# A pipelined scan in a decoder trunk: one pool of raw weights for the whole kernel, and another order of work at the scan's two ends

## The chip, the cores and the metric

The kernel runs on one core of one Trainium2 chip. The metric is device time in microseconds (us) for one execution, and the time given is the median of several executions. One execution is recorded by the hardware profiler; its rows give starts, durations and waits per engine: PE (TensorE), ACT (ScalarE), DVE (VectorE), POOL (GpSimd) and SP (SyncE, which here only issues DMAs).

## The reference

Two layers over 272 tokens (256 and 16 meta tokens) with a model width of 2048, all in float32. Layer 0 is RWKV-7 time mixing and SwiGLU, layer 1 stick-breaking attention and SwiGLU. The change lies in the time mixing:

```python
r = xr @ w_r
k = xk @ w_k
v = xv @ w_v
w = -jax.nn.softplus(-(dec_w0 + jnp.tanh(xw @ dec_w1) @ dec_w2)) - 0.5
decay = jnp.exp(-jnp.exp(w))
a = jax.nn.sigmoid(a_w0 + (xa @ a_w1) @ a_w2)
g = jax.nn.sigmoid(xg @ g_w1) @ g_w2
...
def step(state, inp):
    r_t, d_t, k_t, v_t, kk_t, a_t = inp
    sa = jnp.einsum('bhvk,bhk->bhv', state, -kk_t)
    state = (state * d_t[:, :, None, :]
             + sa[..., None] * (kk_t * a_t)[:, :, None, :]
             + v_t[..., None] * k_t[:, :, None, :])
    return state, jnp.einsum('bhvk,bhk->bhv', state, r_t)

_, y = lax.scan(step, s0, tuple(seq_first(t) for t in (rh, dh, kh, vh, kk, ah)))
...
out = ((y + bonus) * g) @ w_o
```

Behind it come `h = h + mix`, an RMS norm and `(silu(x @ w_gate) * (x @ w_up)) @ w_down`.

## The kernel before

**Weights.** Every weight matrix of 2048 x 2048 is read in 16 column blocks m of 16 row blocks k. A load brings eight blocks of 128 x 128 (512 KB) to a buffer of the pool `wraw`, called `raw`; half of it (four blocks, 128 x 512) is then split in two: ACT casts it to `whi` (fp32r), DVE subtracts to get `wlo`. The activations are split in the same way (`hl`, hi and lo). A block against the 272 tokens is then three matmuls in `mm3k` (lines 186 to 188): hi by hi, lo by hi, hi by lo. There are NWHL = 6 pairs of whi and wlo. The time mixing has NRAW = 3 raw buffers in a pool of its own, which is given back at its end; the rest of the kernel has a second pool of four.

**Stages, with their time in the profiled execution.** The norm, and then k = xk @ w_k (0 to 180 us): the first three column blocks in plain fp32 (line 472), the others split, with the small low-rank matrices (`dec_w1`, `a_w1`, `g_w1`) taken along by `rest()` between the blocks. The key of a block goes through ACT (`kt`, `xi`) to a small matmul `kq` (line 490), which prepares the keys' norm. The scan (180 to about 664 us). Then `wo_first`: the rest of `o @ w_o`, the residual `h` and its squares. From about 690 us FFN, attention and FFN.

**The scan** works on pairs of heads, 16 in all, in chunks of 64 tokens. In iteration n = -3 to 15, four pairs are in hand in different phases: C = pair n+3 (its low-rank terms, `lora`), B = pair n+2 (`chunk0`, `scores`, `solve`, `neg`, `bonus`, `tokens`, `values`), M = pair n+1 (`inverse`, `left`, `right`, `apply`, `trans`: the triangular inverse is done in two levels; its pieces go through DRAM, `s<-G`, `Tt<-s`), and A = pair n (`states`, four times `step`, then `norm` and `gate`, which gives the output o[n]). Between these small pieces `fill` takes steps from `stream`; a step is one weight block, three matmuls. The order of these calls in `scan` sets the order on every engine, and an engine serves its list in that order.

**The stream** delivers, pair by pair, 16 steps of w_v and 16 of w_r, and after the 512th the head of w_o: for m = 0 to 3 the k = 0 to KHEAD-1, as far as o[k] is done, into PSUM banks that stay open (`self.wo`). `chunks` loads its raws, NRAW ahead, and splits one half ahead of its use. The number of steps per iteration is 32; the last three iterations, with no C, call `fill(k / 2)`: 16 steps. 516 steps are taken before those, 48 in them, and 48 w_o steps (4 x 12) stand there.

**`wo_first`** loads k = 12 to 15 of m = 0 to 3 (four raws of 256 KB), does 16 blocks with them and goes on with m = 4 to 15, whose banks are taken in turn from the pool pmm.

SP issues the loads of raw weights, of the lora weights (`w<-lora`, `rn<-rkd`), the transfers through DRAM in the scan, and two stores that zero a DRAM scratch (`s<-zero`); `blk` is a small table of constants, of which ACT makes a scaled copy.

Of the kernel before, what the change touches and what calls it, by code (L numbers as in the profile page):

```python
# [26 lines left out]
C = 64  # L27
# [10 lines left out]
ALIAS = {"kk": "ld"}  # L38
NRAW = 3
NWHL = 6  # L40
NRAW2 = 4
G0 = 3
# [3 lines left out]
NXL = 7  # L46
LEAD = 4
PSTEP = 8
NHEAD = 4
KHEAD = 12  # L50
ASTRIDE = 2
# [67 lines left out]
class Builder:  # L119
# [89 lines left out]

    def proj(self, src, acts, nk=NK, m=128):  # L210
        w = self.weights(src, nk, m)
        out = self.mmbank()[:m, :acts[0][-1].shape[1]]
        for k in range(nk):
            self.mm3k(out, w[k], acts[k], k == 0, k == nk - 1)
        return out
# [45 lines left out]
    def build(self):  # L261
        tc, nc = self.tc, self.nc
        with ExitStack() as ctx:
# [13 lines left out]
            self.wx = None  # L277
            with ExitStack() as c2:
                self.wraw = c2.enter_context(tc.tile_pool(name="wraw", bufs=NRAW))
                self.time_mix()  # L280
            self.wide = True
            if self.stop == "tm":
                return
            with ExitStack() as c2:
                self.wraw = c2.enter_context(tc.tile_pool(name="wraw2", bufs=NRAW2))
                self.consts2 = c2.enter_context(tc.tile_pool(name="cp2", bufs=1)).tile(
# [64 lines left out]
    def time_mix(self):  # L351
# [13 lines left out]
        with ExitStack() as ctx:  # L365
# [8 lines left out]
            for i in range(2):  # L374
                st = {}
                for n, w in (("B0", 64), ("V0", 64), ("SC0", 128)):
                    st[n] = sp.tile([128, w], F32, name=f"{n}_{i}", tag=f"{n}_{i}")
                    nc.gpsimd.memset(st[n], 0.0)
                self.static.append(st)
                z = self.dram.tile([10, 65, 64], F32, name=f"s2_{i}", tag=f"s2_{i}", bufs=1)  # L380
                self.dq.dma_start(z.rearrange("s i t -> (s i t)").rearrange("(p x) -> p x", p=128),
                                  zero)
                self.s2.append(z)
            o, n = CONST["blk"]
            self.blk = [sp.tile([128, n], F32, name="blk", tag=f"blk{i}") for i in range(2)]
            self.dq.dma_start(self.blk[0], a["consts"][:, o:o + n])
            nc.scalar.activation(self.blk[1], self.blk[0], AF.Copy, scale=1.0 / HD)
# [218 lines left out]
    def scan(self, sp):  # L606
# [9 lines left out]
        stream = self.stream(pairs)  # L616
        left = [0]

        def fill(k):
# [7 lines left out]
        for n in range(-3, NK):  # L627
            get = lambda i: pairs.get(n + i)
            A, M, B, C = get(0), get(1), get(2), get(3)
            f = fill if C else lambda k: fill(k / 2)  # L630
            if M:
# [3 lines left out]
            if A:  # L635
                A.states()
                A.step(1)
            if B:
                B.chunk0()
# [15 lines left out]
            if B:  # L655
                B.bonus()
            f(2)
            if B:
                B.tokens()
            f(6 + (LEAD if n == -3 else 0))  # L660
            if B and n + 2 == NK - 1:
# [60 lines left out]
    def chunks(self, jobs):  # L722
# [6 lines left out]
        def load():  # L729
            if len(raws) < len(todo):  # L730
                src, j0, j1 = todo[len(raws)]
                raw = self.wraw.tile([128, (j1 - j0) * 128], F32, name="raw", tag="raw")
                nc.sync.dma_start(raw, src[:, j0 * 128:j1 * 128])
                raws.append(raw)

        def split(raw, k0, k1):
            n = (k1 - k0) * 128
            hi = self.whl.tile([128, n], F32R, name="whi", tag="whi")
            lo = self.whl.tile([128, n], F32R, name="wlo", tag="wlo")
            part = raw[:, k0 * 128:k1 * 128]  # L740
            nc.scalar.copy(hi, part)  # L741
            nc.vector.tensor_tensor(lo, part, hi.bitcast(F32), ALU.subtract)  # L742
            return [(hi[:, k * 128:(k + 1) * 128], lo[:, k * 128:(k + 1) * 128])
                    for k in range(k1 - k0)]

        for _ in range(NRAW):
            load()
        ahead = None
        for i, (src, j0, j1) in enumerate(todo):
# [9 lines left out]
    def stream(self, pairs):  # L759

        a = self.a
        w = self.chunks([(a[n][p], NK) for p in range(NK) for n in ("w_v", "w_r")]
                        + [(a["w_o"][m][:, :KHEAD * 128], KHEAD) for m in range(NHEAD)])
        for p in range(NK):
# [632 lines left out]
```

## Time and profile before

| | us |
|---|---|
| median of three runs | 2739.09 |
| the three runs | 2735.81, 2739.09, 2741.37 |
| the profiled execution | 2735.73 |
| its span, first to last instruction | 2733.9 |
| PE idle over the span | 67.5 |
| PE idle from 178 to 200 us | 10.4 |
| PE idle from 624 to 690 us | 12.6 |

Rows of the time line are: start, duration, engine, line, operation, output <- inputs, size, count, and in brackets the time that the engine stood idle before and what ended that. SPq and ACTq rows are DMAs being issued. A row that stands for several instructions has their number behind the x. A wait list has, for an engine and line, what it waited for: us in all, how often, the longest. A matmul's duration overlaps with its neighbours'; what counts is the time from one start to the next.

### The profile page before, as it was taken

What the parts mean: (1) busy time and instruction counts of PE and PEld (TensorE: products, weight loads), DVE (VectorE), ACT (ScalarE), POOL (GpSimd) and SP (SyncE); (2) the same over time, 40 slices, a digit from 0 to 9 for tenths busy, and PEclk for the clock granted to TensorE, in tenths of its full rate; (3) what the DMA queues carried; (4) which work ended last, traced back from release to release, by engine and by line L of the source; (5) the groups of instructions that cost most, each with busy time, mean ns of one, the idle gap of its engine ahead of it and who ended that gap; (6) DMA issues with size and microseconds to landing.
All of it is one profiled execution on the core that took longest, in us unless ns stands there. A gap on an engine that the chain in (4) does not pass through costs nothing.

```text
span 2733.9 us, 53852 instructions
## 1 busy us (share of the span) xinstructions
PE 2666.4 (98%) x20942; PEld 2464.4 (90%) x20942; DVE 1771.0 (65%) x3543; ACT 1470.0 (54%) x2943; POOL 167.0 (6%) x477
## 2 busy tenths in 40 slices
PE   6989999998999999999999999999999999999999
PEld 4878888887999999999999999988888888888888
DVE  6666666674655555555556775577766666666665
ACT  5665565654554444444445754477555455554553
POOL 0004333331000000000000000000000000000000
PEclk9999999998999999999999999999999999999999
DMA  5434343433655555555555545533555665665655
GB/s 176 137 108 123 92 119 98 119 86 109 197 176 165 185 177 163 186 177 164 185 176 167 181 162 170 170 116 108 186 185 181 197 188 178 198 190 179 199 178 179
DMA packets 185329, 439.50 MB, mean 161 GB/s; under 512 B 58448, under 2 KB 88688, under 8 KB 185072
## 3 DMA queue, kind: packets, MB, share of 16 engines
q1 hardware_dynamic: 183488, 433.63, 50.5%
q8 instruction: 164, 2.69, 0.4%
q10 hardware_dynamic: 1584, 2.42, 0.3%
q14 instruction: 93, 0.76, 0.1%
HBM read 430.24 MB, written 5.74 MB: 159 GB/s over the span
## 4 chain that ended last, share of the span: by engine, by line
PE 75%; DVE 0%; issue 0%
PE mm L192 22%; PE mm L186 13%; PE mm L188 13%; PE mm L187 13%; PE mm L191 11%; PE hms L869 1%; PE z L946 1%; PE lt L959 0%; PE op L970 0%; PE tbv L938 0%; PE op L971 0%; PE lt L960 0%; PE lt L962 0%; PE ms L801 0%; PE op L972 0%; DVE h L208 0%
## 5 line engine op out<-in xcount | busy, mean ns | idle before, releaser
L168 DVE TENSOR_TENSOR wlo<-raw,whi 128x512 fp32r<-128x512 f32 (+1 forms) x1448 | 978.9, 679 | 618.1 <-ACT whi L167 599.2
L167 ACT CAST whi<-raw 128x512 fp32r<-128x512 f32 (+1 forms) x1448 | 879.3, 610 | 870.8 <-PE mm L187 539.6
L186 PE MATMUL mm<-hl,whi 128*128 128x272 f32 x3344 | 982.5, 294 | 14.8 <-ACT whi L741 9.3
L188 PE MATMUL mm<-hl,wlo 128*128 128x272 f32 x3344 | 968.8, 290 | 4.6 <-DVE wlo L168 3.8
L187 PE MATMUL mm<-hl,whi 128*128 128x272 f32 x3344 | 965.8, 289 | 0.0
L192 PE MATMUL mm<-hl,whi 128*128 128x512 f32 x2624 | 919.9, 395 | 0.0
L191 PE MATMUL mm<-hl,wlo 128*128 128x256 f32 x2624 | 740.8, 282 | 0.0
L186 PEld LDWEIGHTS mm<-hl,whi 128*128 128x128 f32 x3344 | 632.0, 189 | 27.5 <-ACT whi L741 9.8
L187 PEld LDWEIGHTS mm<-hl,whi 128*128 128x128 f32 x3344 | 637.8, 191 | 1.9
L188 PEld LDWEIGHTS mm<-hl,wlo 128*128 128x128 f32 x3344 | 631.8, 189 | 7.2 <-DVE wlo L168 4.0
L192 PEld LDWEIGHTS mm<-hl,whi 128*128 128x128 f32 x2624 | 492.5, 188 | 113.0
L191 PEld LDWEIGHTS mm<-hl,wlo 128*128 128x128 f32 x2624 | 494.2, 188 | 0.6
L741 ACT CAST whi<-raw 128x512 fp32r<-128x512 f32 x140 | 83.3, 617 | 63.0 <-PE mm L187 20.1
L742 DVE TENSOR_TENSOR wlo<-raw,whi 128x512 fp32r<-128x512 f32 x140 | 98.7, 712 | 25.7 <-ACT whi L741 25.4
L208 DVE TENSOR_TENSOR h<-h,mm 128x256 f32<-128x256 f32 (+1 forms) x224 | 93.9, 420 | 6.6 <-PE mm L192 6.0
L201 ACT COPY c<-mm 128x256 f32<-128x256 f32 x104 | 38.8, 373 | 79.1 <-PE mm L192 79.0
L1163 POOL TENSOR_TENSOR Tm<-Ts,As 40x14 f32<-40x14 f32 (+6 forms) x224 | 79.1, 353 | 17.6
L186 PE MATMUL mm<-hi,whi 128*128 128x272 f32 x256 | 78.3, 306 | 0.0
L1165 POOL TENSOR_TENSOR Ts<-Ts,Tm 40x14 f32<-40x14 f32 (+6 forms) x224 | 74.9, 334 | 17.5
L187 PE MATMUL mm<-lo,whi 128*128 128x272 f32 x256 | 73.8, 288 | 0.0
L188 PE MATMUL mm<-hi,wlo 128*128 128x272 f32 x256 | 73.5, 287 | 0.0
L186 PEld LDWEIGHTS mm<-hi,whi 128*128 128x128 f32 x256 | 48.1, 188 | 4.4 <-issue 2.4
(277 smaller groups left out, 2275.3 us busy)
## 6 DMA issues: line engine op xcount, KB each, us to landing
raw<-w_gate SPq DMA_DIRECT2D x176, 512.0 KB
raw<-w_up SPq DMA_DIRECT2D x176, 512.0 KB
raw<-w_down SPq DMA_DIRECT2D x128, 512.0 KB
raw<-w_down SPq DMA_DIRECT2D x128, 192.0 KB
raw<-w_v SPq DMA_DIRECT2D x32, 512.0 KB
raw<-w_r SPq DMA_DIRECT2D x32, 512.0 KB
raw<-sb_w_k SPq DMA_DIRECT2D x32, 512.0 KB
raw<-sb_w_v SPq DMA_DIRECT2D x32, 512.0 KB
```

Source lines behind the costliest of these rows:

```text
L167: nc.scalar.copy(hi, part)
L168: nc.vector.tensor_tensor(lo, part, hi.bitcast(F32), ALU.subtract)
L186: mm(out, w[0], x[0], start=first, stop=False)
L187: mm(out, w[0], x[1], start=False, stop=False)
L188: mm(out, w[1], x[0], start=False, stop=last)
L191: mm(out[:, :n], w[1], x[0], start=first, stop=False, skip_group_check=True)
L192: mm(out, w[0], x[2], start=False, stop=last, skip_group_check=True)
L208: self.nc.vector.tensor_tensor(h, h, out[:, c:c + n], ALU.add)
L741: nc.scalar.copy(hi, part)
L742: nc.vector.tensor_tensor(lo, part, hi.bitcast(F32), ALU.subtract)
L1163: V.tensor_tensor(t, Ts[:, 0:i, i:i + 1].to_broadcast([40, i, n]), As[:, i:i + 1, i + 1:].to_broadcast([40, i, n]), ALU.mult)
L1165: V.tensor_tensor(Ts[:, 0:i, i + 1:], Ts[:, 0:i, i + 1:], t, ALU.add)
```

## The change

There is one pool `wraw` of four buffers for the whole kernel. `scan` calls `next(stream)` before `load_low`, which issues the first four loads of w_v and w_r (the stream has yields for this). The zero stores and the load of `blk` are issued by ACT. In the last three iterations `fill(k * 0.625)` takes 20 steps an iteration, 60 in all, and the stream's head of w_o has k = 0 to 12 for four m (52 steps) and then k = 13 and 14 (8 steps, whose raw is made of four 128 KB pieces); the four banks are taken before the first of them, and o[k] is split at its first use. Where B exists but no A (n = -2 and -1), four steps stand before `chunk0` and four fewer behind `tokens`. The two steps between `bonus` and `tokens` are now behind `tokens`. `wo_first` has only k = 15 left, one raw of four 64 KB pieces and twelve matmuls; m = 4 to 7 take the banks of psc and psd.

```diff
-NRAW = 3
+NRAW = 4
 NWHL = 6
-NRAW2 = 4
+DRAIN = 0.625
 NHEAD = 4
-KHEAD = 12
+KHEAD = 13
...
-            with ExitStack() as c2:
-                self.wraw = c2.enter_context(tc.tile_pool(name="wraw", bufs=NRAW))
-                self.time_mix()
+            self.wraw = ctx.enter_context(tc.tile_pool(name="wraw", bufs=NRAW))
+            self.time_mix()
...
-                self.wraw = c2.enter_context(tc.tile_pool(name="wraw2", bufs=NRAW2))
...
-                self.dq.dma_start(z.rearrange("s i t -> (s i t)").rearrange("(p x) -> p x", p=128),
+                nc.scalar.dma_start(z.rearrange("s i t -> (s i t)").rearrange("(p x) -> p x", p=128),
                                   zero)
...
-            self.dq.dma_start(self.blk[0], a["consts"][:, o:o + n])
+            nc.scalar.dma_start(self.blk[0], a["consts"][:, o:o + n])
...
         stream = self.stream(pairs)
         left = [0]
+        next(stream)
...
-            f = fill if C else lambda k: fill(k / 2)
+            f = fill if C else lambda k: fill(k * DRAIN)
...
             if A:
                 A.states()
                 A.step(1)
+            elif B:
+                f(4)
             if B:
                 B.chunk0()
...
             if B:
                 B.bonus()
-            f(2)
             if B:
                 B.tokens()
-            f(6 + (LEAD if n == -3 else 0))
+            f(4 if B and not A else 8 + (LEAD if n == -3 else 0))
...
         for _ in range(NRAW):
             load()
+        yield None
...
-                        + [(a["w_o"][m][:, :KHEAD * 128], KHEAD) for m in range(NHEAD)])
+                        + [(a["w_o"][m][:, :KHEAD * 128], KHEAD) for m in range(NHEAD)]
+                        + [([a["w_o"][m][:, KHEAD * 128:KHEAD * 128 + 256]
+                             for m in range(NHEAD)], 2 * NHEAD)])
+        yield next(w)
...
-        for k in range(KHEAD):
-            self.o.append(self.split(self.oraw[k], self.xs1))
         self.wo = []
         for m in range(NHEAD):
             pool, tag = (self.pmm, "mm") if m < 2 else (self.pfr, "fr")
-            out = pool.tile([128, 512], F32, name="mm", tag=tag)[:, :T]
-            self.wo.append(out)
-            for k in range(KHEAD):
-                self.mm3k(out, next(w), self.o[k], k == 0, False)
-                yield 1
+            self.wo.append(pool.tile([128, 512], F32, name="mm", tag=tag)[:, :T])
+        steps = [(m, k) for m in range(NHEAD) for k in range(KHEAD)]
+        for m, k in steps + [(m, KHEAD + k) for m in range(NHEAD) for k in range(2)]:
+            while len(self.o) <= k:
+                self.o.append(self.split(self.oraw[len(self.o)], self.xs1))
+            self.mm3k(self.wo[m], next(w), self.o[k], k == 0, False)
+            yield 1
...
-        w = [self.weights(a["w_o"][m][:, KHEAD * 128:], NK - KHEAD, 128) for m in range(NHEAD)]
-        for k in range(KHEAD, NK):
-            for m in range(NHEAD):
-                self.mm3k(self.wo[m], w[m][k - KHEAD], self.o[k], False, k == NK - 1)
+        last = [a["w_o"][m][:, (NK - 1) * 128:] for m in range(NHEAD)]
+        raw = self.wraw.tile([128, NHEAD * 128], F32, name="raw", tag="raw")
+        for m in range(NHEAD):
+            nc.sync.dma_start(raw[:, m * 128:m * 128 + 128], last[m])
+        w = self.whl_pair(raw)
+        for m in range(NHEAD):
+            c = slice(m * 128, m * 128 + 128)
+            self.mm3k(self.wo[m], (w[0][:, c], w[1][:, c]), self.o[NK - 1], False, True)
         for m in range(NK):
-            ps = self.wo[m] if m < NHEAD else self.proj(a["w_o"][m], self.o)
+            ps = self.wo[m] if m < NHEAD else self.proj(a["w_o"][m], self.o, late=m < 2 * NHEAD)
```

`proj` takes a bank from psc or psd where `late` is set, and `whl_pair` is the split of a raw (the cast on ACT, the subtraction on DVE) as a function of its own.

On SP, around the last loads of w_k and the first of w_v, the order before is this (`w_2043` and `w_2035` are lora weights of pair 0, `s_0` and `s_1` the DRAM scratch that is zeroed):

```order
L536 DMA raw<-g_w 128x512 x2
L156 DMA raw<-w_k 128x1024 x7
L386 DMA blk<-consts 128x128
L381 DMA s_0_2016<-zero 128x325
L381 DMA s_1_2024<-zero 128x325
L699 DMA rn<-rkd 128x1x272
L733 DMA raw<-w_v 128x1024 x2
L733 DMA raw<-w_r 128x1024
```

With the change it is this:

```order
L543 DMA raw<-g_w 128x512 x2
L156 DMA raw<-w_k 128x1024 x6
L746 DMA raw<-w_v 128x1024 x2
L746 DMA raw<-w_r 128x1024 x2
L706 DMA w_2043<-lora 128x256
L708 DMA rn<-rkd 128x1x272
L746 DMA raw<-w_v 128x1024 x2
```

The first four loads of the stream moved directly behind the last load of w_k, and the stores and blk are gone from this queue. The lora load of pair 0, which stood early in the program, now stands here.

On ACT, at the scan's start, the order before is this (`rk` is the keys' norm, `ld`, `ta`, `P`, `pe` and `Q` belong to pair 0's decay and rates, `ARV` and `V` take the projected values):

```order
L499 ACT_TABLE_LOAD
L499 ACTIVATE rk<-kqs 32x272
L387 ACTIVATE blk<-blk 128x128
L500 ACT_TABLE_LOAD
L500 ACTIVATE rk<-rk 32x272
L1031 ACTIVATE P<-L 128x16
L1032 ACTIVATE P<-L 128x4x64
L1034 ACTIVATE pe<-L 128x4
L1037 ACTIVATE Q<-L,dv 128x272
L741 CAST whi<-raw 128x512 x10
```

With the change:

```order
L388 DMA s_0_2016<-zero 128x325
L507 ACT_TABLE_LOAD
L507 ACTIVATE rk<-rk 32x272
L388 DMA s_1_2024<-zero 128x325
L393 DMA blk<-consts 128x128
L1040 ACTIVATE ld<-zw,dv 128x272
L394 ACTIVATE blk<-blk 128x128
L1044 ACTIVATE ta<-za,dv 128x272
L1090 COPY V_0_2012<-mm 128x16
L1091 COPY ARV<-mm 128x4x64
L1047 ACTIVATE P<-L 128x16
```

Six casts of the stream now stand before these rows, between those of w_k. The two stores and the blk load are issued between the table loads, and the copy of blk stands two rows behind its load.

On ACT, at the scan's end, the order before is this (the last three state copies `S` of pair 15, its group norm `rs`, the split `hl` of o[15], then casts of w_o):

```order
L1311 ACTIVATE S<-cb,pe 128x64 x3
L1315 ACTIVATE sq<-cb 128x272
L1317 COPY y<-cb 128x272
L1325 ACT_TABLE_LOAD
L1325 ACTIVATE rs_9389<-vb,dv 128x272
L1326 ACT_TABLE_LOAD
L1326 ACTIVATE rs_9389<-rs_9389 128x272
L288 DMA consts_9460<-consts 128x1056
L249 CAST hl<-o 128x272
L167 CAST whi<-raw 128x512 x6
```

With the change:

```order
L1327 ACTIVATE S<-cb,pe 128x64 x3
L1331 ACTIVATE sq<-cb 128x272
L1333 COPY y<-cb 128x272
L167 CAST whi<-raw 128x512
L1341 ACT_TABLE_LOAD
L1341 ACTIVATE rs_9444<-vb,dv 128x272
L1342 ACT_TABLE_LOAD
L1342 ACTIVATE rs_9444<-rs_9444 128x272
L167 CAST whi<-raw 128x512
L295 DMA consts_9521<-consts 128x1056
L167 CAST whi<-raw 128x512 x2
L258 CAST hl<-o 128x272
```

The four casts for m = 4 stand ahead of the split of o[15]; the cast for k = 15 (one) and those for k = 13 and 14 stand further ahead.

More of the change, by code (lines that the diff above doesn't have):

```diff
@@ L208, in added, with whl_pair, proj @@
             self.nc.vector.tensor_tensor(h, h, out[:, c:c + n], ALU.add)
-    def proj(self, src, acts, nk=NK, m=128):
+    def whl_pair(self, part):
+        nc = self.nc
+        n = part.shape[1]
+        hi = self.whl.tile([128, n], F32R, name="whi", tag="whi")
+        lo = self.whl.tile([128, n], F32R, name="wlo", tag="wlo")
+        nc.scalar.copy(hi, part)
+        nc.vector.tensor_tensor(lo, part, hi.bitcast(F32), ALU.subtract)
+        return hi, lo
+    def proj(self, src, acts, nk=NK, m=128, late=False):
         w = self.weights(src, nk, m)
-        out = self.mmbank()[:m, :acts[0][-1].shape[1]]
+        out = (self.scbank("mm") if late else self.mmbank())[:m, :acts[0][-1].shape[1]]
         for k in range(nk):
@@ L732, in load @@
                 raw = self.wraw.tile([128, (j1 - j0) * 128], F32, name="raw", tag="raw")
-                nc.sync.dma_start(raw, src[:, j0 * 128:j1 * 128])
+                if isinstance(src, list):
+                    for i, x in enumerate(src):
+                        nc.sync.dma_start(raw[:, i * 256:i * 256 + 256], x)
+                else:
+                    nc.sync.dma_start(raw, src[:, j0 * 128:j1 * 128])
                 raws.append(raw)
         def split(raw, k0, k1):
[L737 to L742, printed above, removed]
+            hi, lo = self.whl_pair(raw[:, k0 * 128:k1 * 128])
             return [(hi[:, k * 128:(k + 1) * 128], lo[:, k * 128:(k + 1) * 128])
```

## The prediction

> **What bounds the kernel now.** I read the page first, for the engine that fills the span, and then its windows by stage.
>
> ```profile
> span 2733.9 us, 53852 instructions
> PE 2666.4 (98%) x20942; PEld 2464.4 (90%) x20942; DVE 1771.0 (65%) x3543; ACT 1470.0 (54%) x2943; POOL 167.0 (6%) x477
> ```
>
> TensorE (PE) is busy 98% of the span. All its idle time is 2733.9 - 2666.4 = 67.5 us, so no change of order can bring more than that plus what it gives back in clock. The windows say where it lies (length, then busy us of PE, PEld, DVE, ACT, POOL, granted clock, DMA share, GB/s):
>
> ```profile
> 57.00:178.00 121.00, 116.19 (x767) 101.50 (x768) 76.53 (x165) 80.87 (x184) 0.00 (x0) 1.00 0.36 114
> 178.00:200.00 22.00, 11.61 (x66) 10.56 (x65) 11.39 (x27) 12.14 (x24) 1.06 (x9) 0.69 0.57 183
> 225.00:230.00 5.00, 3.20 (x45) 2.81 (x44) 3.28 (x8) 2.02 (x4) 3.91 (x11) 0.72 0.02 8
> 230.00:610.00 380.00, 370.34 (x4932) 328.56 (x4925) 258.51 (x661) 222.68 (x534) 144.47 (x406) 1.00 0.37 107
> 624.00:690.00 66.00, 53.37 (x542) 47.77 (x543) 32.87 (x75) 30.21 (x62) 9.00 (x25) 0.84 0.39 128
> 690.00:2733.90 2043.90, 2040.40 (x14046) 1914.59 (x14045) 1334.91 (x2462) 1071.89 (x2018) 0.00 (x0) 1.00 0.56 175
> ```
>
> From 690 us on PE is idle 3.5 us out of 2043.9, at full clock: three quarters of the span cannot gain from this change, which removes no matmul. What can be won is at the scan's two ends: 10.4 us idle in 178 to 200 and 12.6 us in 624 to 690, both with a lowered clock as well. Between them, in 380 us of steady scan, 9.7 us are idle.
>
> **1. Start and w_k (0 to 178 us).** With four raw buffers and the small lora load moved behind, weights land earlier. Two rows at the start show what is traded:
>
> ```profile
> 23.21 0.41 ACT L707 CAST w2h<-w 128x256 fp32r<-128x256 f32 x1 [5.05 <-DMA w<-lora]
> 54.03 0.39 PE L186 MATMUL mm<-hl,whi 128*128 128x272 f32 x1 [1.65 <-ACT kt L483]
> ```
>
> The cast of the lora weights, for which ACT waited 5.05 us with the norm's Ln queued behind, goes; in its place ACT and DVE get casts of w_k inside the chain of the norm, a whi of about 0.62 and two wlo of about 0.69 us (durations below), so the first w_k matmul comes later by up to 2 us. The wait of 1.65 us at 54.03, behind a whi that itself waited for its transfer, should go. I take 0 for both; between +2 and -1.7 us.
>
> In the w_k loop PE waits for `kq`, whose input stands on ACT behind casts that wait for transfers (the wait list first, then ACT, then PE at the largest):
>
> ```profile
> PE kq L490 <- ACT xi L487: 4.7, 5, 1.6
> 119.79 0.62 ACT L167 CAST whi<-raw 128x512 fp32r<-128x512 f32 x1 [5.08 <-DMA raw<-w_k]
> 121.30 0.65 PE L490 MATMUL kq<-xi,consts 128*32 128x272 f32 x2 [1.64 <-ACT xi L487]
> ```
>
> ACT waits 5.08 us for a w_k half that SP could not request, since three buffers held older blocks. With the fourth, both halves of a block stand ahead of the three lora loads on SP. The DMA share of 0.36 in this window leaves room to send them. Of 4.7 us I take **3** (0 to 4.7). Six casts of the stream's first blocks are new on ACT and DVE here, 6 x 0.62 = 3.7 us on ACT; it is busy 80.87 of 121 us, so there is cover, but it keeps me from taking all 4.7.
>
> **2. Scan start (178 to 200 us).** SP first, then ACT, then PE:
>
> ```profile
> 180.63 0.82 SPq L733 DMA_DIRECT2D raw<-w_v  x2
> 180.61 1.28 ACT L499 ACT_TABLE_LOAD   x1
> 188.85 3.66 ACT L741 CAST whi<-raw 128x512 fp32r<-128x512 f32 x6 [3.65 <-DMA raw<-w_v]
> 177.76 0.29 PE L187 MATMUL mm<-hl,whi 128*128 128x272 f32 x1
> 178.26 0.29 PE L188 MATMUL mm<-hl,wlo 128*128 128x272 f32 x1
> 189.52 0.59 PE L186 MATMUL mm<-hl,whi 128*128 128x272 f32 x1 [9.30 <-ACT whi L741]
> 191.16 0.60 PE L188 MATMUL mm<-hl,wlo 128*128 128x272 f32 x1 [0.81 <-DVE wlo L742]
> 191.78 0.43 PE L187 MATMUL mm<-hl,whi 128*128 128x272 f32 x1
> 196.31 0.35 PE L186 MATMUL mm<-hl,whi 128*128 128x272 f32 x1
> ```
>
> The first w_v load is issued at 180.63, behind the prologue's last loads and stores, and PE stands still 9.30 + 0.81 = 10.1 us. Then the clock is low: 20 matmuls start in 196.31 - 191.78 = 4.53 us, 0.226 each, against (178.26 - 177.76) / 4 = 0.125 before. For the 24 matmuls up to 196.31 that is an excess of 24 x 0.10 = 2.4 us. Together 12.5 us.
>
> After: six casts (6 x 4 blocks x 3 matmuls x 0.125 = 9 us of PE work) stand ahead of this point, so PE runs until about 179.9 + 9 = 189. The next whi stands on ACT behind two table loads of 1.28 us, the two zero stores and the blk load that ACT now issues, and the blk copy, which waits for blk to land. Before, ACT had done with this chain at 188.85 - 3.65 = 185.2; the new wait for blk is between 0 and about 3.65 us (what a raw load cost at 188.85). Then whi and wlo, 1.3 us: 186.5 to 190.2, against 189. I take a left-over stall of 1.5 us (0 to 4), without a low clock after it. Gain **11** (7 to 12.5).
>
> **3. First pairs (200 to 230 us).**
>
> ```profile
> 217.24 4.67 SPq L733 DMA_DIRECT2D raw<-w_r  x2
> 225.25 1.87 ACT L741 CAST whi<-raw 128x512 fp32r<-128x512 f32 x3 [2.72 <-DMA raw<-w_r]
> 226.83 0.30 PE L1090 MATMUL z<-AR,B 64*64 64x32 f32 x4 [1.80 <-POOL Tm L1163]
> ```
>
> The window 225 to 230 has 1.8 us idle at a clock of 0.72, another 1.4 us: 3.2 in all. ACT was late for a w_r half whose request stood 4.67 us on SP. One raw more ahead, and four stream steps (1.5 us of PE) before `chunk0` of the first two pairs, cover it. I take **2.5** (0 to 3.2).
>
> **4. Steady scan.** The number of stream steps per iteration is the same. New is only that the two steps between `bonus` and `tokens` now follow `tokens`. The transposes write banks that others must have read (ACT, then PE):
>
> ```profile
> 588.66 0.48 ACT L1028 ACTIVATE ta<-za,dv 128x272 f32<-128x272 f32 x1
> 590.18 0.32 PE L1190 MATMUL tv<-consts,ARV 128*64 128x128 f32 x1
> ```
>
> The last reader near them ends at 588.66 + 0.48 = 589.14; without the two steps (6 x 0.125 = 0.75 us) `tv` would start at 589.4. So no wait: **0** (-2 to +2 over all iterations).
>
> **5. Tail (624 to 690 us).** From the wait list a group of short waits, then one matmul at the low clock, PE's longer waits, what they hang on, and the windows at low clock:
>
> ```profile
> PE cb L1309 <- ACT S L1311: 2.5, 6, 0.4
> 637.15 0.43 PE L187 MATMUL mm<-hl,whi 128*128 128x272 f32 x1
> 639.85 0.44 PE L1228 MATMUL yb<-Tt,An 64*64 64x64 f32 x2 [1.36 <-DMA Tt<-s]
> 667.78 0.60 PE L186 MATMUL mm<-hl,whi 128*128 128x272 f32 x1 [3.14 <-ACT whi L167]
> 669.36 0.59 PE L186 MATMUL mm<-hl,whi 128*128 128x272 f32 x1 [0.76 <-ACT whi L167]
> 681.65 0.59 PE L188 MATMUL mm<-hl,wlo 128*128 128x272 f32 x1 [3.79 <-DVE wlo L168]
> 662.42 1.78 SPq L156 DMA_DIRECT2D raw<-w_o  x4
> 658.02 0.31 ACT L1311 ACTIVATE S<-cb,pe 128x64 f32<-128x64 f32 x1 [0.55 <-PE cb L1309]
> 667.03 0.44 DVE L250 TENSOR_TENSOR hl<-o,hl 128x272 fp32r<-128x272 f32 x1 [0.48 <-ACT hl L249]
> 667.76 0.69 DVE L168 TENSOR_TENSOR wlo<-raw,whi 128x512 fp32r<-128x512 f32 x1 [0.29 <-ACT whi L167]
> 636.80:646.80 10.00, 8.33 (x58) 7.13 (x57) 2.19 (x6) 4.10 (x5) 0.00 (x0) 0.50 0.20 57
> 667.70:674.00 6.30, 5.46 (x22) 5.14 (x23) 2.75 (x4) 1.90 (x5) 0.00 (x0) 0.50 0.95 312
> 681.60:684.10 2.50, 2.45 (x11) 2.45 (x12) 2.50 (x5) 0.60 (x3) 0.00 (x0) 0.50 0.26 93
> ```
>
> The four waits are 1.36 + 3.14 + 0.76 + 3.79 = 9.05 us. At the half clock half of the busy time is excess: 4.2 + 2.7 + 1.2 = 8.1. Together 17.1 us. The wait at 639.85 goes: 20 instead of 16 steps an iteration put 4 x 0.375 = 1.5 us more ahead of it. The one at 681.65 goes: m=4 has its own banks, and its raws no longer wait for the release that let SP issue only at 662.42. The one at 667.78 stays in another form. Pair 15's last output, o[15], was split at 667.47, 9.1 us after the last state copy ended (658.33), and PE had run dry at 664.6. Five steps more stand after that copy (12 added in all, the other 7 ahead of it), so PE lasts 5 x 0.375 = 1.9 us longer. But DVE now makes two wlo (2 x 0.69) inside o[15]'s chain, and the twelve matmuls for it stand ahead of m=4 on PE: a stall of 3.14 - 1.9 + 1.4 = 2.6, say 3 us with ACT's extra whi. Of the 8.1 us of low clock I leave 3.5, one stretch behind either wait. Gain 17.1 - 3 - 3.5 = **10.5** (5 to 14).
>
> A page of the Trainium skill weighs against the loads of k=15, four pieces of 64 KB: DMA: Bandwidth & Descriptors, section Bandwidth, calls for batches of 1 MiB and gives 0.95 us for 64 KB, by which an estimate for four is 3.8 us. No run here shows it; the pieces are requested while twelve steps are still to run, so the sum would be the same.
>
> **Sum:** 0 + 3 + 11 + 2.5 + 0 + 10.5 = 27 us. The profiled execution took 2735.73 us, 1.8 more than its span, and lies 3.4 below the median of the three runs, 2739.09. From it the sum gives 2708.7, from the median **2712 us**, which I predict (1.0% less).
>
> **Rivals.**
> - *The stalls only move.* ACT serves its work in order, so blk's landing (up to 4 us before the next whi) and o[15]'s chain decide, each with a low-clock stretch behind it (2.4 us). For it: both stand on ACT and DVE in the new order. Against it: six casts are done beforehand. Gain 3 + 6 + 0 + 5 = 14: 2725 us. Chance 0.22.
> - *No low-clock stretch is left*, and the upper ends hold: 1.7 + 4 + 12 + 3 + 14 = 35: 2704 us. Chance 0.15. Against it: the clock was low at 637.15 already, ahead of the wait at 639.85, where the only waits are those for the state copies, none over 0.4 us. Short waits are enough, by this row. The Trainium skill (TensorE: Matmul & The Clock Gate, practical table at its end) asks only that no idle gap between matmuls be over about 3 us; by this rule the time would come out near this rival's. The row at 637.15 disagrees.
> - *The change doesn't do what it says:* the fourth buffer is not free in time, since DVE's casts release it late, and w_v still lands after 185. Then only the m=4 wait and the one at 639.85 go, about 5 us: 2734 us. Chance 0.05.
> - *Slower: `tokens` lost its cover.* If in each of 16 pairs the transposes wait for ACT or DVE, 0.75 us is lost, and if the clock then drops for a stretch (3.4 us at half speed costs 1.7), 2.45. Times 16 that is 39, less 27: 12 us slower, 2751. It decides from 27 / 16 = 1.7 us a pair. Against it speaks the margin at 589.14 to 589.4, and that the window 230 to 610 kept a clock of 1.00 with 9.7 us of waits. Chance 0.03.
>
> **How the numbers follow.** The forecast has 0.55 with 2704 to 2719 as its own range. About 0.2% (5.5 us) can be told from no change. Faster: 0.55 + 0.22 + 0.15 = 0.92; same 0.05; slower 0.03. The range reaches from the upper bounds of all terms (1.7 + 4.7 + 12.5 + 3.2 + 14 = 36 us, 2703) to the first rival with 3 us less (2728): it leaves out the two last rivals and some of the first, 0.15.
>
> **What would show it.** Right: SP issues w_v before 175 us; the wait at the scan's first stream matmul falls from 9.30 to under 4; `kq` waits under 2 in all; no wait at `yb` for Tt in the tail; one wait of 2 to 4 us at k=15 and none at m=4. Wrong: the steady window 230 to 610 has over 12 us idle, or the first w_k matmul starts over 2 us later, or low-clock stretches as many as before.

## The result and the profile after

The changed kernel took 2712.57 us (median of five, 2708.42 to 2714.09) against 2736.78 us for the kernel before (median of five, 2735.81 to 2741.37, the three runs shown above among them). The ratio is 0.9906, with a 95% interval of 0.9891 to 0.9920: 24 us, about 1%, faster. The profiled execution has a span of 2712.2 us against 2733.9, so 21.7 us are there to be found in the two traces.

Five places of the program, the same in both kernels, cut that sum into stages: the last low-rank matmul `za` of pair 0 ends the w_k stage; the first state-copy matmul (`cb<-S,Mp`) of pair 0, of pair 12, and the end of the span. First the changed kernel's rows, then those of the kernel before that were not shown yet.

```profile
span 2712.2 us, 53883 instructions
176.06 0.29 PE L188 MATMUL za<-a_w1h,w2l 96*128 96x272 f32 x1
243.99 0.33 PE L1325 MATMUL cb<-S,Mp 64*64 64x64 f32 x4
577.82 0.33 PE L1325 MATMUL cb<-S,Mp 64*64 64x64 f32 x4
```

```profile
179.01 0.28 PE L188 MATMUL za<-a_w1h,w2l 96*128 96x272 f32 x1
253.22 0.33 PE L1309 MATMUL cb<-S,Mp 64*64 64x64 f32 x4
583.83 0.33 PE L1309 MATMUL cb<-S,Mp 64*64 64x64 f32 x4
```

| stage | before, us | after, us | gain | forecast |
|---|---|---|---|---|
| start and w_k, to `za` | 179.01 | 176.06 | 2.95 | 0 + 3 |
| scan start and first pairs, to pair 0's states | 74.21 | 67.93 | 6.28 | 11 + 2.5 |
| twelve iterations, pair 0 to pair 12 | 330.61 | 333.83 | -3.22 | 0 |
| tail and all behind it | 2150.07 | 2134.38 | 15.69 | 10.5 |
| sum | 2733.9 | 2712.2 | 21.7 | 27 |

The wait list of PE in the changed kernel, up to 700 us, without the waits of the start, and the windows as for the kernel before. (`Tt` is the piece of a pair's triangular inverse that comes back from DRAM; `yb` and `zb` are small matmuls of the inverse, and `Ys` is what DVE makes of `yb` for `zb`.)

```profile
PE zb L1263 <- DVE Ys L1249: 9.6, 14, 0.9
PE yb L1244 <- DMA Tt<-s: 3.5, 2, 3.2
PE kq L497 <- ACT xi L494: 2.9, 2, 1.6
...
PE mm L186 <- ACT hl L258: 2.0, 1, 2.0
...
```

```profile
178.00:200.00 22.00, 19.22 (x167) 18.25 (x166) 14.68 (x36) 12.75 (x29) 0.00 (x0) 0.92 0.40 132
225.00:230.00 5.00, 3.77 (x30) 3.54 (x31) 1.60 (x4) 0.00 (x0) 0.00 (x0) 0.66 0.36 65
230.00:610.00 380.00, 367.14 (x4958) 325.38 (x4956) 254.17 (x648) 224.66 (x530) 145.70 (x406) 1.00 0.37 107
624.00:690.00 66.00, 61.13 (x612) 57.33 (x611) 39.86 (x88) 37.78 (x75) 2.80 (x11) 0.97 0.57 175
```

The wait of 9.30 us at the stream's first cast is down to 2.05, that of 3.79 at m = 4 is gone, and one wait of 2.0 us (for `hl`, the split of o[15]) is left behind the scan. Against that, 225 to 230 us is as low in clock as before, with a wait for Tt of 3.2 us that reaches into it, and the steady scan has 12.9 us idle instead of 9.7: the waits at `zb` for Ys went from 3.0 us to 9.6 in all.

### The profile page after: what moved, and what is told of

Read it like the earlier page. It is cut to its first block, busy times and chain, and to the rows that moved or that the text cites. A ratio compares the mean times of both kernels' runs of the same rounds, so it can differ in the third digit from the quotient of the medians.

```text
span 2712.2 us, 53883 instructions
## 1 busy us (share of the span) xinstructions
PE 2655.1 (98%) x20942; PEld 2456.4 (91%) x20942; DVE 1769.2 (65%) x3546; ACT 1477.1 (54%) x2946; POOL 167.6 (6%) x477
## 4 chain that ended last, share of the span: by engine, by line
PE 92%; DVE 3%; DMA 2%; ACT 2%; issue 1%; POOL 0%; SPq 0%; ACTq 0%; POOLq 0%; DVEq 0%
PE mm L192 22%; PE mm L186 16%; PE mm L188 16%; PE mm L187 16%; PE mm L191 11%; DMA raw<-w_k 1%; PE lr L549 1%; PE mm L479 1%; PE cb L1325 1%; DVE wlo L216 1%; PE wa L1274 1%; PE hms L885 1%; PE cb L1317 1%; PE z L962 1%; ACT L1342 0%
## 5 line engine op out<-in xcount | busy, mean ns | idle before, releaser
L168 DVE TENSOR_TENSOR wlo<-raw,whi 128x512 fp32r<-128x512 f32 (+1 forms) x1444 | 977.0, 679 | 623.2 <-ACT whi L167 603.6
L167 ACT CAST whi<-raw 128x512 fp32r<-128x512 f32 (+1 forms) x1444 | 880.0, 612 | 863.5 <-PE mm L187 545.5
L215 ACT CAST whi<-raw 128x512 fp32r<-128x512 f32 (+1 forms) x147 | 88.7, 609 | 74.0 <-PE mm L187 65.9
L216 DVE TENSOR_TENSOR wlo<-raw,whi 128x512 fp32r<-128x512 f32 (+1 forms) x147 | 102.5, 707 | 39.7 <-ACT whi L215 31.8
```

## The experiments

Ten of the kernels ran once each, so they are read by rows and by the time from one row to another, not by totals. How steady such readings are shows in the runs that leave a part alone: `za` came at 174.56 to 177.87 us (nine runs), pair 0's states 65.7 to 69.4 us behind it (seven), the twelve iterations took 333.8 to 334.9 us (nine), and from pair 12's states to the end it took 2134.0 to 2136.4 us (six). Smaller differences than that are not taken for effects. Of the kernel before there is one trace.

**The stall left at the scan's start.** In the changed kernel it looks like this, on ACT and then on PE:

```profile
179.87 0.59 ACTq L393 DMA_DIRECT2D blk<-consts  x1
185.70 0.31 ACT L394 ACTIVATE blk<-blk 128x128 f32<-128x128 f32 x1 [4.12 <-DMA blk<-consts]
```

```profile
188.21 0.39 PE L186 MATMUL mm<-hi,whi 128*128 128x272 f32 x1 [2.05 <-ACT whi L215]
189.46 0.60 PE L188 MATMUL mm<-hi,wlo 128*128 128x272 f32 x1 [0.73 <-DVE wlo L216]
```

ACT stands 4.12 us at the copy of blk, and everything behind it, P and Q and the next four casts, is later by that. The edit:

```diff
-nc.scalar.dma_start(self.blk[0], a["consts"][:, o:o + n])
-nc.scalar.activation(self.blk[1], self.blk[0], AF.Copy, scale=1.0 / HD)
+nc.gpsimd.tensor_tensor(self.blk[1], self.cst("ident"), self.cst("cen"), ALU.subtract)
+nc.gpsimd.tensor_scalar(self.blk[0], self.blk[1], float(HD), None, ALU.mult)
```

> The block table blk is computed on POOL from two tables that are in SBUF already (ident minus cen, times 64), so neither its load nor its copy stands on ACT; all else is as in the changed kernel. Theory A (the rest of the stall at the scan's start is the 4.12 us that ACT waited for blk to land, behind the stream's 512 KB loads): the wait of 2.05 + 0.73 us at PE's seventh stream half is gone or under 0.5 us, no low clock at 188 to 192, and the first state-copy matmul of pair 0 comes 3 to 4.5 us earlier than 243.99. Rival (the stall is ACT's and DVE's own work there, table loads, P, Q and casts): the wait shrinks by less than 1 us.

The window and the row of pair 0's states in this kernel:

```profile
178.00:200.00 22.00, 22.00 (x209) 21.13 (x208) 18.54 (x48) 15.02 (x37) 0.00 (x0) 1.00 0.45 136
238.96 0.33 PE L1325 MATMUL cb<-S,Mp 64*64 64x64 f32 x4
```

PE has no idle time and full clock there, and pair 0's states come 5.0 us earlier. Counted from `za` (175.57 in this run) it is 63.4 us instead of 67.9, and 2.3 us less than the shortest of the seven runs above. Theory A holds; the rival falls.

**The steady scan.** Two experiments, one that moves the DVE work and one that takes the fourth buffer away:

```diff
+    def out(self):
...
+        V.scalar_tensor_tensor(y, y, self.vec("mgn"), self.bv, ALU.mult, ALU.add)
+        o = b.kp.tile([128, T], F32, name="o", tag="kp")
+        V.scalar_tensor_tensor(o, y, self.vec("gn_b"), self.gp[:, :T], ALU.add, ALU.mult)
...
                 M.left(32)
+            if A:
+                A.out()
```

> The last two DVE operations of a pair's output (y times gain plus bonus, and o) are emitted behind left(32), so that Ys stands ahead of them on DVE as before the change; no other order is touched on PE or SP. Theory B (the steady scan lost 0.27 us an iteration because one more DVE operation of 0.5 us stands ahead of the second Ys): the waits for Ys in 230 to 610 fall from 8.6 to about 3 us, an iteration takes 27.55 us instead of 27.82, total 3 us less than the changed kernel. Rival (the two stream steps that were taken out from between bonus and tokens): the period stays at 27.8.

```diff
-NRAW = 4
+NRAW = 3
```

> Three raw buffers instead of four, in the whole kernel (so the FFN has one less than both kernels had; read the scan only). Theory B (the fourth buffer shifts the stream's splits against the pair's work, and by it the order on DVE): period 27.55 us as before the change, Ys waits about 3 us. Theory on the w_k loop (the fourth buffer lets SP request the second half of w_k earlier): the last low-rank matmul za of pair 0 ends the w_k stage at about 178, not at 176.06, with kq waits back at 4 to 5 us. At the scan's start three raws instead of four are ahead: the stall there grows by 2 to 5 us. Rival for the w_k stage (the moved small load at the start did it): 176 as with four.

DVE in one iteration around the second Ys: the kernel before, then the changed kernel, then the one with `out` behind left(32).

```profile
491.49 0.53 DVE L1330 TENSOR_TENSOR y<-y,rs 128x272 f32<-128x272 f32 x1
491.93 0.41 DVE L1233 TENSOR_TENSOR Ys<-yb,consts 128x256 f32<-128x256 f32 x1
492.27 0.56 DVE L1331 SCALAR_TENSOR_TENSOR y<-y,dv,bv 128x272 f32<-128x272 f32 x1
```

```profile
484.27 0.78 DVE L216 TENSOR_TENSOR wlo<-raw,whi 128x512 fp32r<-128x512 f32 x1
484.97 0.52 DVE L1347 SCALAR_TENSOR_TENSOR y<-y,dv,bv 128x272 f32<-128x272 f32 x1
485.42 0.41 DVE L1249 TENSOR_TENSOR Ys<-yb,consts 128x256 f32<-128x256 f32 x1
```

```profile
483.98 0.41 DVE L1251 TENSOR_TENSOR Ys<-yb,consts 128x256 f32<-128x256 f32 x1
484.31 0.55 DVE L1360 SCALAR_TENSOR_TENSOR y<-y,dv,bv 128x272 f32<-128x272 f32 x1
PE zb L1265 <- DVE Ys L1251: 4.3, 12, 0.5
```

With the change, an operation of 0.5 us that nobody waits for soon (`y<-y,dv,bv`) slipped ahead of Ys, which PE needs for the next `zb`. Behind Ys again, the twelve iterations take 329.65 us (from 245.78 to 575.43), 27.47 each instead of 27.82, and the wait falls from 8.6 to 4.3 us. With three buffers they take 330.81 (from 245.49 to 576.30), 27.57 each, although the two stream steps are where the change put them. So theory B holds and the moved steps are not the cause. On the w_k stage the three-buffer run settles nothing: `za` came at 177.39, inside the spread, although the waits for `kq` were 5.6 us (4.7 in the kernel before, 1.5 to 3.9 in the runs with four buffers). Its stall at the scan's start, 2.51 + 0.73 us, is hardly longer than with four, against the 2 to 5 us more that were expected.

**The wait for Tt.**

```diff
-            elif B:
-                f(4)
...
-            f(4 if B and not A else 8 + (LEAD if n == -3 else 0))
+            f(8 + (LEAD if n == -3 else 0))
```

> In the iterations n = -2 and -1 no stream steps stand ahead of chunk0; all eight stand behind tokens. Theory C (pair 0's chain from its scores through POOL and DRAM to Tt takes a fixed time of about 20 us, and the four steps ahead of chunk0 start it 1.5 us later against PE's other work): the wait for Tt at yb falls from 3.23 to about 1.7 us, the wait at za (1.24) may go up to 1 us, pair 0's first state copy comes 1 to 2 us earlier than 243.99. Rival (the steps give w_r time to land, as the forecast had it): the wait moves ahead to chunk0, 1.5 to 3 us, and nothing is gained or up to 1.5 us lost.

The changed kernel (the first matmul of pair 0's scores, then the two waits), the same kernel when it ran again for the last comparison below, and this one:

```profile
197.17 0.37 PE L1126 MATMUL ba<-ARV,BK 64*128 64x128 f32 x1
218.49 0.39 PE L186 MATMUL za<-a_w1h,w2h 96*128 96x272 f32 x1 [1.24 <-ACT BV L1116]
226.01 0.30 PE L1244 MATMUL yb<-Tt,An 64*64 64x64 f32 x2 [3.23 <-DMA Tt<-s]
```

```profile
224.16 1.45 PE L1244 MATMUL yb<-Tt,An 64*64 64x64 f32 x15 [1.66 <-DMA Tt<-s]
```

```profile
224.76 0.30 PE L1242 MATMUL yb<-Tt,An 64*64 64x64 f32 x2 [1.39 <-DMA Tt<-s]
225.32 0.62 PE L1242 MATMUL yb<-Tt,An 64*64 64x64 f32 x13 [0.27 <-DMA Tt<-s]
```

The wait at `za`, which is 0.9 to 1.9 us in every run of the new order with the four steps, is gone. The waits at `yb` are 1.66 us, as theory C had it (1.7), but the changed kernel itself waited 1.66 us there when it ran again, so this fall is not shown to come from the edit. Pair 0's states come 1.15 us earlier and 66.3 us behind `za`, inside the spread, so a worth in time is not shown either. The chain is longer than the theory's 20 us: in the changed kernel it takes 28.8 us from the first matmul of pair 0's scores to `yb`, 13 of them on POOL (208.23 to 221.29). That the four steps ahead of `chunk0`, which the forecast counted as a gain, start this chain later shows only where the wait for blk is gone: behind `za` the scores start at 16.6 us with blk on POOL alone (192.14 - 175.57) and at 15.1 us with all repairs (191.81 - 176.75). Pair 0's states are 0.4 us apart in these two.

**The start.**

```diff
...
+                ins = A.mul(u, hn[k][:, :T], self.vec(f"mu{i}", k))
+                if i == 2 and k == 5:
+                    self.hold = ins
...
+                if m == G0:
+                    with tc.issue_after(self.hold.ins):
+                        p = self.proj(a["w_k"][m], xk)
...
```

> The four casts of the first split w_k block (m = 3) are held back on ACT until the sixth mix of the start; all else is as in the changed kernel. Theory D (with four buffers this block's raws land early, and ACT puts its cast, which waits 3.15 us for the transfer, between the norm's Ln and Exp; the moved lora load alone had gained 3.4 us here, which this gives back): the first w_k matmul comes at 24.3 to 24.6 instead of 28.71, and the last low-rank matmul za of the w_k stage at 171.5 to 173.5 instead of 176.06. Rival (the w_k loop is paced by the raw transfers, so what is won at the start is lost in its waits for kq, as with three buffers, where the first matmul came at 24.30 and za at 177.39): za stays within 1 us of 176.06.

On ACT of the changed kernel (the first two rows), and on PE of this one:

```profile
20.12 0.49 ACT L432 ACTIVATE rstd<-ss,dv 128x272 f32<-128x272 f32 x1 [2.07 <-PE ss L427]
23.76 0.62 ACT L167 CAST whi<-raw 128x512 fp32r<-128x512 f32 x1 [3.15 <-DMA raw<-w_k]
```

```profile
24.17 6.22 PE L481 MATMUL mm<-xi,raw 128*128 128x272 f32 x18 [4.24 <-DVE xi L443]
50.61 0.39 PE L186 MATMUL mm<-hl,whi 128*128 128x272 f32 x1 [2.34 <-ACT kt L492]
178.01 0.29 PE L188 MATMUL za<-a_w1h,w2l 96*128 96x272 f32 x1
```

The windows from the first w_k matmul to `za`, in the changed kernel and in this one:

```profile
28.71:176.06 147.35, 143.69 (x883) 123.20 (x884) 101.61 (x221) 104.89 (x240) 0.40 (x3) 1.00 0.40 128
24.17:178.01 153.84, 147.29 (x883) 125.37 (x884) 103.17 (x223) 106.25 (x242) 0.41 (x3) 0.98 0.39 125
```

The mechanism is as theory D says: the first matmul comes 4.5 us earlier, 24.17 instead of 28.71. But `za` comes at 178.01, 1.95 us later and not earlier, which is at the edge of the spread and more than the 1 us that the rival allowed. The w_k stage gives the 4.5 us back and more: it is idle 6.55 us instead of 3.66, 2.34 of them at 50.61, and at a clock of 0.98 instead of 1.00 PE is busy 3.6 us longer with the same matmuls. The rival is right that nothing is won; that the transfers set the pace, its reason, is not shown.

**The place of the first loads on SP.**

```diff
-        next(stream)
...
         self.load_low(None, pairs[0])
+        next(stream)
```

> The stream's first four raw loads are issued behind the lora load and rn of pair 0 on SP instead of ahead of them. In the changed kernel rn was issued at 174.13, ten microseconds after the load ahead of it, so SP stood in wait there. Theory G (what counts at the scan's start is the place on SP): the first w_v load is issued at 174.5 to 175.5, PE waits 2 to 5 us for the stream's first half at 177 to 182, and pair 0's first state copy comes 2 to 5 us later than 243.99. Rival (the fourth buffer and the removed stores suffice): it comes within 1 us.

SP of this kernel, then ACT, then PE:

```profile
173.38 0.65 SPq L708 DMA_DIRECT2D rn<-rkd  x1
174.14 0.86 SPq L746 DMA_DIRECT2D raw<-w_v  x2
```

```profile
182.60 0.31 ACT L394 ACTIVATE blk<-blk 128x128 f32<-128x128 f32 x1 [2.99 <-DMA blk<-consts]
183.56 0.62 ACT L215 CAST whi<-raw 128x512 fp32r<-128x512 f32 x1
```

```profile
184.23 0.59 PE L186 MATMUL mm<-hl,whi 128*128 128x272 f32 x1 [7.70 <-ACT whi L215]
252.92 0.33 PE L1325 MATMUL cb<-S,Mp 64*64 64x64 f32 x4
```

Theory G holds in its direction; the size, 8.9 us, is nearly twice the upper end of what was expected. The stream's loads now stand behind a small load (`rn`), on a queue that stood still until 173.38. But the 8.9 us are not the place on SP alone: the cast that PE waits 7.70 us for did not wait for its raw. It stood on ACT behind the copy of blk, for which ACT waited 2.99 us. How much of the loss is left without blk was not tried.

**The tail.** Four experiments, each with one part of the tail as before. First the old banks (`late` left out), then the old number of steps (DRAIN 0.5, KHEAD 12, four raws of 256 KB behind the scan), then two pools, and last the kernel before with nothing but one pool of four.

```diff
-            ps = self.wo[m] if m < NHEAD else self.proj(a["w_o"][m], self.o, late=m < 2 * NHEAD)
+            ps = self.wo[m] if m < NHEAD else self.proj(a["w_o"][m], self.o)
```

> The column blocks m = 4 to 7 of w_o take their banks in turn from pmm and pfr as before, not from psc and psd. Theory E (the wait of 3.79 us at m = 4 went because of the banks of its own): a wait of 2 to 4 us comes back at the first matmul of m = 4 or m = 5, for an h addition on DVE, and the time grows by 2 to 6 us with the low clock behind it. Rival (it went because the raws no longer wait for the release of the scan's pools, so the splits are ahead): no new wait, time within 1 us.

```diff
-DRAIN = 0.625
+DRAIN = 0.5
...
-KHEAD = 13
+KHEAD = 12
...
```

> 48 steps of w_o in the tail as before (half the rate, k = 0 to 11), k = 12 to 15 in the code after the scan with their four raws of 256 KB, but the one pool, the early loads and the banks of m = 4 to 7 as in the changed kernel. Theory F (most of the tail's gain of 15.7 us is work that now stands where PE waited): the wait for Tt at yb in the tail comes back with 1 to 1.5 us and a low-clock stretch behind it is likely, and the wait at the first block after the scan is 3 to 5 us instead of 2.01; the time grows by 4 to 9 us. Rival (the pool and the banks made the gain): it grows by less than 2 us.

```diff
-            self.wraw = ctx.enter_context(tc.tile_pool(name="wraw", bufs=NRAW))
-            self.time_mix()
+            with ExitStack() as c2:
+                self.wraw = c2.enter_context(tc.tile_pool(name="wraw", bufs=NRAW))
+                self.time_mix()
...
+                self.wraw = c2.enter_context(tc.tile_pool(name="wraw2", bufs=NRAW))
```

> As the changed kernel, but with two pools of four raws, the second taken after the scan's pools are given back, as before. The two tail runs so far cost little each (from the first state copy of pair 12 to the end: 2134 to 2136 us where the tail is untouched, 2136.3 with the old banks, 2137.4 with the old rate, 2150.1 in the kernel before). Theory H (the first loads of w_o after the scan waited for that release, and this is most of the tail's 15.7 us): the load of k = 15 is issued only after the last activation of pair 15, PE waits 4 to 8 us there, and that length is 2141 to 2147 us. Rival (the 12 steps more, the banks and the pool cover for one another, none alone holds the gain): it is 2135 to 2139 us.

```diff
-NRAW = 3
+NRAW = 4
...
-                self.wraw = c2.enter_context(tc.tile_pool(name="wraw2", bufs=NRAW2))
```

> The kernel before with one change: one pool of four raws for all of it (no loads ahead of the lora load, the old places of blk and the stores, 48 steps, k = 12 to 15 after the scan, the old banks). Theory H: from pair 12's first state copy to the end 2137 to 2142 us instead of 2150.1, with no wait over 2 us at m = 4. Theory B predicts an iteration of 27.8 us in the steady scan by the fourth buffer alone, instead of 27.55. At the scan's start the wait of 9.3 us stays within 2 us. Rival for the tail (banks and steps are needed): 2145 us or more.

| from pair 12's states to the end | us |
|---|---|
| kernel before | 2150.07 |
| before, with one pool of four | 2137.6 |
| changed, old number of steps | 2137.4 |
| changed, two pools | 2136.5 |
| changed, old banks | 2136.3 |
| changed, tail untouched (six runs) | 2134.0 to 2136.4 |

The lengths are differences of rows, as above (for the fourth, 2714.9 - 578.41). In the kernel with one pool only, the first loads for the code behind the scan on SP, the waits on PE, and a window of the tail:

```profile
621.30 5.09 SPq L156 DMA_DIRECT2D raw<-w_o  x2
...
664.77 0.39 PE L186 MATMUL mm<-hl,whi 128*128 128x272 f32 x1 [1.15 <-ACT hl L249]
672.52 0.39 PE L188 MATMUL mm<-hl,wlo 128*128 128x272 f32 x1 [1.05 <-DVE wlo L168]
...
610.00:690.00 80.00, 72.54 (x819) 64.90 (x816) 45.06 (x102) 43.98 (x89) 9.94 (x29) 1.00 0.50 153
```

One pool of four alone brings 12.4 of the 15.7 us: SP issues the first w_o load for the code behind the scan at 621.30 there instead of 662.42, and the waits of 3.14 and 3.79 us shrink to 1.15 and 1.05, at full clock. The edit does two things at once, a fourth buffer in the scan and no release of the pool behind it. The time at which SP can issue speaks for the release: theory H is right that the tail of the kernel before waited for it.

In the other direction, taking the one pool away from the changed kernel gives 2136.5 us, 0.1 above the untouched runs. The load of k = 15 on SP, in the changed kernel and with two pools:

```profile
633.84 2.68 SPq L823 DMA_DIRECT2D raw<-w_o  x4
644.39 2.87 SPq L825 DMA_DIRECT2D raw<-w_o  x4
```

The load comes 10.6 us later, but not behind pair 15's last activation (658.95), as was expected. A cast on ACT waits 3.10 us for it, and the state copy behind that cast makes PE wait 1.67 us at 650.03 instead of 0.41; at k = 15 itself the wait is 1.34 us, less than the 2.0 of the changed kernel. So this edit does not bring back the late release of the kernel before, where SP could issue only at 662.42. One difference is that both pools have four buffers here, where the kernel before had three and four; whether that is why was not tried. What so late a release would cost with the twelve more steps stays open.

The old banks bring back a wait of 1.24 us at m = 4, less than expected, and no length outside the spread. The old number of steps gives waits of 1.0 us at `yb` and 1.15 at the first block, at full clock, and a length 1.0 us above the spread. Theory F fell, and of E only the wait is there. The one-pool run also has 27.81 us per iteration (from 248.79 to 582.46), so the fourth buffer alone brings the slower steady scan, and it keeps a wait of 8.4 us at the scan's start.

**All repairs together.** blk on POOL, `out` behind left(32), no steps ahead of `chunk0`; and the changed kernel again on the same chip:

> The changed kernel with blk computed on POOL, the last two DVE operations of a pair behind left(32), and no steps ahead of chunk0. If the three costs found add up (5.0 us at the scan's start, 0.3 us in each of 12 iterations, about 1 us at za and yb): 8 to 10 us less than the changed kernel, 2702 to 2706 us. If the chain through POOL and DRAM takes back what comes earlier (yb waits longer by as much): 4 to 6 us less.

> The changed kernel once more, on the same chip as the combined one, for the comparison: 2708 to 2715 us.

| | median, us | range | ratio to before |
|---|---|---|---|
| kernel before (nine runs) | 2734.73 | 2732.39 to 2737.50 | |
| changed kernel again | 2718.03 | 2714.13 to 2719.59 | 0.9936 (0.9924 to 0.9949) |
| with the repairs | 2702.67 | 2700.88 to 2706.59 | 0.9882 (0.9867 to 0.9897) |

The repaired kernel is the fastest, and its range lies wholly below that of the changed one. The changed kernel gained 0.6% here where the first comparison gave 0.9%, and their intervals do not quite meet: from one comparison to the next the ratio moves by some 0.3%. With 2718.03 us it also lies above the 2708 to 2715 that were expected. The two profiled executions differ by 7.5 us (spans of 2704.8 and 2712.3): 5.4 in twelve iterations, 2.3 up to pair 0's states, and 0.2 the other way behind them. `za` came 2.2 us later in the repaired one (176.75 against 174.56), so behind `za` it is 4.5 us, as with blk alone. The third repair added nothing that shows: PE, earlier by what blk gave, waits 2.6 us for Tt at `yb` again. The medians are 15.4 us apart, twice the 7.5 of the traces: the repaired kernel's profiled execution was the slowest of its four, the other one (2714.16) next to the fastest of its five. The rows account for the 7.5 us alone.

## Why the prediction came out right, point by point

The time was met almost to the microsecond, but not by its terms: of 27 us forecast the traces show 21.7, with two stages too high and one too low, and the median of before came down by 2.3 us with two more runs. By the medians the gain was 24.2 us. That these errors left 0.6 us between forecast and time is luck; the same kernel took 2718.03 us when it ran again.

- **Start and w_k.** The sum was right (2.95 for 3), but the spread between runs is 3.3 us, so two traces can't confirm it. Its two signs were right as well: without the lora cast the first w_k matmul came at 24.30 instead of 27.72 us (in the run with three buffers), and with the casts of w_k inside the norm's chain it came at 28.71, since ACT waited 3.15 us for the transfer where the prediction counted only the casts' own time. The waits for `kq` fell by 1.8 us (4.7 to 2.9) of the 3, and not to the 2 that it gave as a sign. That the sum is good owes something to the w_k stage, which swallows gains at the start.
- **Scan start.** The mechanism was right, and the term was mis-sized: 1.5 us of stall left over and no low clock behind it was the step that failed. The stall was 2.05 + 0.73 = 2.78 us, and the clock fell. With 1.5 us for the low clock (an estimate, 0.39 of the first window's 4 us), about 8 us of the 12.5 were won, not 11, which is inside the term's range:

```profile
188.00:192.00 4.00, 3.06 (x13) 2.84 (x14) 4.00 (x12) 3.16 (x8) 0.00 (x0) 0.61 0.25 53
226.00:230.00 4.00, 3.77 (x30) 3.52 (x31) 1.60 (x4) 0.00 (x0) 0.00 (x0) 0.57 0.31 50
```

  The wait for blk was 4.12 us, above the bound of 3.65 taken from a raw's wait; this is what the first rival had named. At its other place, the chain of o[15], a wait of 2.01 us stayed, which the forecast had left there.
- **First pairs.** Wrong. The step "one raw more ahead, and four stream steps ahead of `chunk0`, cover it" saw the wait for POOL's `Tm` as a matter of weights that came late. It was the chain itself, 28.8 us from pair 0's scores through POOL and DRAM to Tt. PE comes there earlier, and the wait moves to `yb` (3.23 us, 1.66 when the kernel ran again). The four steps stand ahead of the scores, where the chain begins, and so cover nothing of it; a new wait of 1.24 us at `za`, for ACT, came with them. With some 8 us won at the scan's start, the 6.28 us of the stage leave about -2 for this term instead of +2.5 (an estimate by difference).
- **Steady scan.** Wrong in the step that looked for a cost only where the code was moved: it cost 3.22 us, and the sign of being wrong, over 12 us idle from 230 to 610, appeared with 12.9. The margin at `tokens` was there, as argued, and that rival did not occur. What came was another order on DVE, brought by the fourth buffer; three rows of DVE's list for one iteration, of before and of the change, would have told it.
- **Tail.** Better than forecast. The waits went as said, with 2.0 us instead of 3 left at o[15]. But the account by parts was wrong: it gave each wait to one edit, where one pool of four alone brings 12.4 of the 15.7 us.

The Trainium skill (TensorE: Matmul & The Clock Gate, practical table at its end) asks for no idle gap over about 3 us. The first window above shows the low clock behind gaps of 2.05 and 0.73 us, so the trace disagrees. The wait of 3.23 us ahead of the second window agrees. Nor does the length of a gap settle it: with three buffers, gaps of 2.51 and 0.73 us at the same place (190.02 and 191.26) were followed by the full clock.

```profile
186.00:200.00 14.00, 10.74 (x108) 9.67 (x108) 9.82 (x25) 7.96 (x22) 0.00 (x0) 1.00 0.30 96
```

## What to carry to other kernels

A strict queue makes a small load dear: one table of 64 KB, issued behind large loads and read by an engine that feeds everything else, cost 4 to 5 us, and the place of the stream's first loads on SP, together with a wait for that table, cost 9. What can be computed from data at hand, or asked for earlier, should be. Where a wait is the end of a chain through several engines, work that is moved ahead of its start does not cover it; find where the chain begins before filling in front of it. And a change of a buffer count reorders the engines' lists everywhere that a scheduler decides, so compare one steady iteration on each engine, not only the places edited, and count overlapping edits together: two that cover the same wait do not add.

## What the runs showed of the hardware

The load of blk, 64 KB, was issued at 179.87 us, and ACT could go on with it only at 185.70, 5.2 us after the issue ended, though it went out on ACT's own queue and not on SP's. In those microseconds large raw loads were being moved at 339 GB/s:

```profile
180.00:184.00 4.00, 4.00 (x35) 4.00 (x34) 2.52 (x6) 1.57 (x3) 0.00 (x0) 1.00 0.89 339
```

Two stores of 162.5 KB went out on ACT's queue just ahead of it, and could be the cause as well. In the run with the stream's loads behind `rn`, blk was issued at 175.31, ahead of both stores but behind the first raw loads, and ACT could go on with it only at 182.60, 6.95 us after the issue ended. So the stores are not needed for the delay. In the kernel before it was issued on SP ahead of the stores and the raw loads (177.45) and used without a wait at 182.24, so it was there 4.5 us after its issue ended at the latest. That the large loads held blk up fits all three, but was not tried by itself; another issuing engine, at least, gave it no quick way.
